# Attention's product with the values over four query blocks at once, with less descriptor scratch and another staging of branch A

## The chip, the cores and the metric

The kernel runs on one core of a Trainium2 chip. The metric is the device time of one execution in microseconds (us), given as the median of several runs. The kernel's engines are named as the profile names them: PE is TensorE's matmul row, PEld its weight loads, DVE is VectorE, ACT is ScalarE, POOL is GpSimd, and SP is the engine whose queue issues most of the DMAs.

## The reference

One layer of a hybrid encoder, on one sequence of 1024 tokens with 1024 channels, all in float32:

```python
h = rmsnorm(x, ln1_g) * (1 + sc1) + sh1
q, k, v, cb, cc, cx, ga, gb = split(h @ w_in)          # 16 heads of 64 channels for q, k, v
z = (rmsnorm(q) . rmsnorm(k)) / sqrt(64)               # strictly causal, 128-query blocks
A[t,s] = sigmoid(z_ts) * prod_{s<j<t} (1 - sigmoid(z_tj)),  s < t
y_a = A @ v                                            # per head
y_b = cb * causal_dwconv3(cc * cx)
merged = sigmoid(ga) * (y_a @ w_branch_a) + sigmoid(gb) * (y_b @ w_branch_b)
x = x + g1 * (merged @ w_out)
h = rmsnorm(x, ln2_g) * (1 + sc2) + sh2
x = x + g2 * ((silu(h @ w_gate) * (h @ w_up)) @ w_down)
```

sh1, sc1, g1, sh2, sc2 and g2 come from a product of silu(c) with a weight matrix.

## The kernel before

Every float32 product is made from a high and a low part of each operand, so a product of two split operands takes three matmuls (high by high, high by low, low by high). The stages follow each other: the input projections, attention together with branch B, branch A, the output projection, and the channel sub-layer with its two products. A matmul's moving operand is 512 columns wide nearly everywhere.

The change lies in the stage of attention. The generator `attention()` walks over 16 heads by 8 blocks of 128 queries; one pair of a head h and a block i is a step, s = 8h + i. In step s it issues

- the scores of its own block (`att_scores`, lines 921 and 922: `z` in two banks of PSUM, then ACT's sigmoid into a row tile `pt`, then a mask by POOL),
- the transposes of the block two steps earlier (`att_trans`, line 950: chunks of up to four 128x128 blocks into the PSUM tile `tr`; ACT copies the high part to `ath`, line 953, and DVE writes the low part to `atl`, line 954),
- the scan of its own block (`att_scan`, line 936 on DVE, and a product on POOL that finishes `pt`),
- in every second step the product with the values (`att_av`, lines 965 and 966), three steps behind (DAV = 3).

In `att_av` the stationary operand is `vt`, the 128 keys by 64 differences of neighbouring values, as 64 high and 64 low columns. The moving operand is a block of `ath` or `atl`: 128 keys by the queries of two blocks, 256 columns, and 128 columns for the last key block, which only the second of the two query blocks sees. The sums lie in the PSUM tile `o`. Two ACT instructions add the last value to the upper half (`otmp`, line 970), a DVE instruction adds the lower half (`oy`, line 972), and a DMA on SP's queue stores 64 channels by 256 queries in `d_ya` (line 974).

Each step's yields carry costs. The main loop adds them up and, in proportion, issues pieces of `fillers()` on PE: first conv B (the projection for cb, whose result is split into `ybh` and `ybl` and stored), then branch B's projection (lines 1026 to 1028, `pj`). A yield of 0 buys no piece before the last block; after it (`flush`), every yield buys 1.3 units, two pieces of three 512-column matmuls. PE's instructions, and those of DVE and POOL that belong to attention, are then chained in the order written (`in_order`); ACT, SP and the other DVE instructions are placed by the scheduler.

After attention, branch A's operand is read back: 16 loads `yr<-d_ya` on SP's queue (line 1173), each split by ACT (line 1176) and DVE into a tile `ya` that takes the place of an attention tile no longer used (`slots`). Pair (n, k) is half n of the queries and channel group k, that is heads 2k and 2k + 1; (1, 7) needs the last head's last product. Branch A multiplies these (`mm_ch`): its first two groups sum in the banks of `z`.

The pool `bp` holds the tiles of attention, `fp` those of fillers and staging, `fq` the tiles `ybh` and `ybl`. Meanwhile `mods_last` fetches 16 tiles `ad` of modulation weights by DMAs from POOL's queue, three buffers deep, and `preload_wo` splits the first weights of the output projection (line 1162) once those tiles are free.

Of the kernel before, what the change touches and what calls it, by code (L numbers as in the profile page):

```python
# [9 lines left out]
F32 = mybir.dt.float32  # L10
F32R = mybir.dt.float32r
AF = mybir.ActivationFunctionType
ALU = mybir.AluOpType
# [4 lines left out]
P = 128  # L18
# [4 lines left out]
DH = 64  # L23
# [7 lines left out]
def block_kernel(tc, x, x_t, cols, ada_1, ada_2, ada_row, w_q, w_kv, w_cg, w_a, w_b, w_o, w_g, w_u, w_d, out):  # L31
    nc = tc.nc
# [7 lines left out]
    def nm(s):  # L40
        uid[0] += 1
        return f"{s}_{uid[0]}"
# [29 lines left out]
    d_ya = [drp.tile([P, KT, 512], F32, name=f"d_ya{n}") for n in range(2)]  # L72
# [64 lines left out]
    pps = psA.enter_context(tc.tile_pool(name="psA", bufs=1, space=PSUM, reuse_waits="tile"))  # L137
# [759 lines left out]
    first_at = (at_tile("ath"), at_tile("atl"))  # L897
# [42 lines left out]
    def att_trans(h, i):  # L940
        pt, off = ptof.pop((h, i)), D - (i + 1) * P
        for b0 in range(0, i + 1, 4):
            nb = min(4, i + 1 - b0)
            key = (h, i // 2, b0 // 4)
            if key not in ats:
                ats[key] = (at_tile("ath"), at_tile("atl")) if ats else first_at
            th, tl = ats[key]
            tr = pps.tile([P, 512], F32, tag="tr", bufs=NTR, name=nm("tr"))
            for j in range(nb):
                nc.tensor.transpose(tr[:, j * P:(j + 1) * P], pt[:, off + (b0 + j) * P:off + (b0 + j + 1) * P], ident)  # L950
            c0 = (i % 2) * P
            src = tr[:, :nb * P].rearrange("p (j t) -> p j t", t=P)
            nc.scalar.activation(th[:, :nb, c0:c0 + P], src, AF.Copy)  # L953
            nc.vector.tensor_tensor(out=tl[:, :nb, c0:c0 + P], in0=src, in1=th[:, :nb, c0:c0 + P].bitcast(F32),  # L954
                                    op=ALU.subtract)
            yield F_T * nb

    def att_av(h, g):
        pr, e0 = h // 2, (h % 2) * DH
        vt = vts[h]  # L960
        o = pps.tile([P, 256], F32, tag="o", bufs=1, name=nm("o"))
        for j in range(2 * g + 2):
            c0 = P if j == 2 * g + 1 else 0
            th, tl = ats[h, g, j // 4]
            nc.tensor.matmul(o[:, c0:], vt[:, j, :], th[:, j % 4, c0:], start=(j == 0), stop=False)
            lastav[0] = nc.tensor.matmul(o[:, c0:], vt[:, j, :], tl[:, j % 4, c0:], start=False, stop=(j == 2 * g + 1))  # L966
        tmp = bp.tile([DH, 256], F32, tag="otmp", bufs=1, name=nm("otmp"))
        yv = bp.tile([DH, 256], F32, tag="oy", bufs=3, name=nm("oy"))
        for e in range(2):
            nc.scalar.activation(tmp[:, e * P:(e + 1) * P], o[:DH, e * P:(e + 1) * P], AF.Identity,  # L970
                                 bias=vlast[:, h, 2 * g + e:2 * g + e + 1])
        nc.vector.tensor_tensor(out=yv, in0=o[DH:], in1=tmp, op=ALU.add)
# [8 lines left out]
    def attention():  # L981

        steps = [(h, i) for h in range(H) for i in (LAST if h == H - 1 else ORDER)]
        for s in range(len(steps) + DAV):
# [27 lines left out]
            yield from av_  # L1012
# [118 lines left out]
    fqpool.close()  # L1131


    sml = ExitStack()
    mlp = sml.enter_context(tc.tile_pool(name="mlp", bufs=1, side="right", reuse_waits="tile"))
# [16 lines left out]
    def preload_wo():  # L1152

        wx = swx.enter_context(tc.tile_pool(name="wpx", bufs=1, side="right", reuse_waits="tile"))
        for j in range(3):
# [3 lines left out]
            for k in range(nk):  # L1159
# [7 lines left out]
    slots = [("va", 1), ("vb", 1), ("skl", 2), ("sq", 2), ("skh", 2), ("vt", 2), ("skl", 2), ("sq", 2), ("skh", 2),  # L1167
             ("ath", 3), ("atl", 3), ("ath", 3), ("atl", 3), ("ath", 3), ("atl", 3), ("vt", 2)]
    yah, yal = ([[None] * KT for n in range(2)] for e in range(2))
    with tc.high_priority():  # L1170
        for (tag, bufs), (n, k) in zip(slots, [(0, k) for k in range(7)] + [(1, 0), (1, 1), (1, 2), (0, 7)] + [(1, k) for k in range(3, 8)]):
            yr = fp.tile([P, 512], F32, tag="yr", bufs=3, name=nm("yr"))
            nc.sync.dma_start(yr, d_ya[n][:, k, :])
            ya2 = bp.tile([P, 2, 512], F32R, tag=tag, bufs=bufs, name=nm("ya"))
            h_, l_ = ya2[:, 0], ya2[:, 1]
            nc.scalar.activation(h_, yr, AF.Copy)
            tt(nc.vector, l_, yr, h_.bitcast(F32), ALU.subtract)
            yah[n][k], yal[n][k] = h_, l_
    mh, mlo = [None] * 2, [None] * 2
# [611 lines left out]
```

## Time and profile before

| what | value |
|---|---|
| median of 3 runs | 1793.41 us (1792.94 to 1793.71) |
| the profiled execution | 1792.41 us |
| its span, first to last instruction | 1790.4 us |
| granted TensorE clock | 1.000 |
| PE busy | 1782.5 us |
| PEld busy | 1485.4 us |
| DVE busy | 1273.5 us |
| ACT busy | 830.9 us |
| POOL busy | 345.0 us |

The median stands 1.0 us above the profiled execution, and that one 2.0 us above its span. Matmuls overlap in the pipeline: the profile gives each a start and a modelled end, so the mean duration of a 512-column matmul (389 ns) is longer than the distance from its start to the next start. What a matmul costs PE is that distance. Attention runs from 596 to 978 us of the span.

### The profile page before, as it was taken

The numbers are of one execution on the slowest core, as the hardware profiler recorded it, in microseconds if no ns is written. First come the engines' busy times: TensorE is split into PE (matmuls) and PEld (weight loads), VectorE is DVE, ScalarE is ACT, GpSimd is POOL, SyncE is SP. The second block draws the span as 40 slices with busy tenths as digits, with TensorE's granted clock in tenths as the row PEclk, the third lists the DMA queues.
The fourth block names the chain that finished last, engine by engine and source line by source line (L and its number), as shares of the span: only waits on it lengthen the run. The fifth ranks groups of instructions, "written<-read, shape, count | busy, mean of one in ns | idle before, by whom it ended". The sixth has DMA issues, their size and how long they took to land.

```text
span 1790.4 us, 24937 instructions
## 1 busy us (share of the span) xinstructions
PE 1782.5 (100%) x8611; PEld 1485.4 (83%) x8611; DVE 1273.5 (71%) x2030; ACT 830.9 (46%) x1555; POOL 345.0 (19%) x437
## 2 busy tenths in 40 slices
PE   9999999999999999999999999999999999999999
PEld 7888877888888888888888888888888888888887
DVE  6876586777874678777786864698867777644876
ACT  5534364333433567776675221764544444422321
POOL 0024334734231334333332100100000000000000
PEclk9999999999999999999999999999999999999999
DMA  9479654222634977796655856424534344389876
GB/s 383 162 248 381 240 185 165 77 94 100 225 130 147 298 197 191 218 324 172 166 136 176 308 194 212 129 95 169 208 130 148 147 183 157 137 316 345 276 236 220
DMA packets 165010, 359.09 MB, mean 201 GB/s; under 512 B 15538, under 2 KB 60938, under 8 KB 163732
## 3 DMA queue, kind: packets, MB, share of 16 engines
q1 hardware_dynamic: 128300, 289.65, 49.1%
q10 hardware_dynamic: 33096, 55.25, 8.7%
q0 software_dynamic: 3488, 12.59, 2.0%
q8 instruction: 69, 1.13, 0.3%
q14 instruction: 57, 0.47, 0.1%
HBM read 247.84 MB, written 109.62 MB: 200 GB/s over the span
## 4 chain that ended last, share of the span: by engine, by line
PE 96%; DMA 1%; DVE 1%; issue 0%; ACT 0%; POOL 0%; SPq 0%; POOLq 0%; DVEq 0%; ACTq 0%
PE e L129 8%; PE e L128 8%; PE e L127 8%; PE pj L127 7%; PE pj L128 7%; PE pj L129 7%; PE pj L294 7%; PE pj L1026 5%; PE pj L1028 5%; PE pj L1027 5%; PE e L1618 4%; PE e L1619 4%; PE e L1620 4%; PE tr L950 3%; PE o L966 2%; PE z L921 2%
## 5 line engine op out<-in xcount | busy, mean ns | idle before, releaser
L1234 ACT ACTIVATE whi<-raw 128x512 fp32r<-128x512 f32 x137 | 84.9, 628 | 160.6 <-PE e L128 99.8
L1235 DVE TENSOR_TENSOR wlo<-raw,whi 128x512 fp32r<-128x512 f32 x137 | 93.1, 687 | 70.6 <-ACT whi L1234 53.1
L133 POOL TENSOR_TENSOR pt<-pt 128x63 f32<-128x63 f32 (+7 forms) x128 | 101.6, 794 | 212.1 <-DVE pt L936 195.7
L128 PE MATMUL e<-big,whi 128*128 128x512 f32 x352 | 136.9, 389 | 0.0
L127 PE MATMUL e<-big,whi 128*128 128x512 f32 x352 | 136.5, 390 | 0.0
L129 PE MATMUL e<-big,wlo 128*128 128x512 f32 x352 | 136.1, 389 | 0.0
L294 PE MATMUL pj<-whi,big 128*128 128x512 f32 x448 | 132.6, 393 | 0.6 <-ACT big L263 0.4
L133 DVE TENSOR_TENSOR c<-pj,c 128x512 f32<-128x512 f32 x140 | 93.7, 684 | 53.9 <-PE pj L129 53.3
L954 DVE TENSOR_TENSOR atl<-tr,ath 128x512 fp32r<-128x512 f32 (+1 forms) x192 | 104.1, 553 | 35.6 <-ACT ath L953 34.2
L127 PE MATMUL pj<-big,whi 128*128 128x512 f32 x320 | 124.9, 390 | 0.0
L129 PE MATMUL pj<-big,wlo 128*128 128x512 f32 x320 | 124.7, 390 | 0.0
L128 PE MATMUL pj<-big,whi 128*128 128x512 f32 x320 | 124.6, 389 | 0.0
L1619 PE MATMUL e<-wlo,f 128*128 128x512 f32 (+1 forms) x319 | 121.9, 382 | 0.0
L1618 PE MATMUL e<-whi,f 128*128 128x512 f32 (+1 forms) x319 | 121.7, 382 | 0.0
L1620 PE MATMUL e<-whi,f 128*128 128x512 f32 (+1 forms) x319 | 121.6, 382 | 0.0
L923 ACT ACTIVATE pt<-z,rq 128x128 f32<-128x128 f32 (+1 forms) x192 | 107.2, 578 | 26.3 <-PE z L922 23.8
L524 ACT ACTIVATE whi<-raw 128x512 fp32r<-128x512 f32 x108 | 67.5, 629 | 109.0 <-PE pj L128 54.3
L133 DVE TENSOR_TENSOR wlo<-raw,whi 128x512 fp32r<-128x512 f32 x108 | 89.4, 831 | 36.2 <-ACT whi L524 36.1
L1026 PE MATMUL pj<-big,whi 128*128 128x512 f32 x256 | 113.3, 442 | 0.0
L953 ACT ACTIVATE ath<-tr 128x512 fp32r<-128x512 f32 (+1 forms) x192 | 93.2, 488 | 31.8 <-PE tr L950 30.8
L127 PE MATMUL e<-rh,whi 128*128 128x512 f32 x264 | 102.7, 389 | 0.0
L128 PE MATMUL e<-rl,whi 128*128 128x512 f32 x264 | 102.7, 389 | 0.0
(304 smaller groups left out, 4756.1 us busy)
## 6 DMA issues: line engine op xcount, KB each, us to landing
f<-d_f SPq DMA_DIRECT2D x77, 512.0 KB, 4.2
d_f<-fs SPq DMA_DIRECT2D x70, 512.0 KB, 2.6
raw<-w_cg SPq DMA_DIRECT2D x40, 512.0 KB, 4.1
raw<-w_u SPq DMA_DIRECT2D x26, 512.0 KB, 4.5
raw<-w_g SPq DMA_DIRECT2D x25, 512.0 KB, 3.4
raw<-w_kv SPq DMA_DIRECT2D x20, 512.0 KB, 5.2
ld<-ada SPq DMA_DIRECT2D x16, 512.0 KB, 8.7
d_t<-ts SPq DMA_DIRECT2D x16, 512.0 KB, 6.7
```

The lines of the kernel that those rows point to most:

```text
L127: nc.tensor.matmul(ps, wh[:, k, :], fh[:, k, :], start=(k == 0 and not onto), stop=False, skip_group_check=onto)
L128: nc.tensor.matmul(ps, wh[:, k, :], fl[:, k, :], start=False, stop=False, skip_group_check=onto)
L129: last = nc.tensor.matmul(ps, wl[:, k, :], fh[:, k, :], start=False, stop=(k == 3), skip_group_check=onto)
L133: eng.tensor_tensor(out=out, in0=a, in1=b, op=op)
L294: nc.tensor.matmul(ps, a, b, start=(k == 0 and q == 0), stop=(k == KT - 1 and q == 2))
L923: nc.scalar.activation(pt[:, off + s0:off + s0 + m], z[:, :m], AF.Sigmoid, scale=rq[:, 1, i, h:h + 1])
L953: nc.scalar.activation(th[:, :nb, c0:c0 + P], src, AF.Copy)
L954: nc.vector.tensor_tensor(out=tl[:, :nb, c0:c0 + P], in0=src, in1=th[:, :nb, c0:c0 + P].bitcast(F32), op=ALU.subtract)
L1026: nc.tensor.matmul(ps, wh, rh_, start=(k == 0), stop=False)
L1618: nc.tensor.matmul(o, sh, w[0][:, c], start=(j == 0), stop=False)
L1619: nc.tensor.matmul(o, sh, w[1][:, c], start=False, stop=False)
L1620: nc.tensor.matmul(o, sl, w[0][:, c], start=False, stop=(j == NJ - 1))
```

## The change

`att_av` now takes four query blocks at once. It is called for i = 3 and i = 7 of a head in place of i = 1, 3, 5 and 7. For key blocks that all four query blocks see, the moving operand has 512 columns; for the four diagonal key blocks it has 512, 384, 256 and 128. It is issued in pieces of two key blocks, with yields of 0 between. In the steps with s % 8 = 6 the first piece stands behind the first chunk of transposes, the rest at the end of the step. For the second half of a head the first two pieces stand at the end of the step with s % 8 = 2, the third piece behind the first chunk of transposes of the next step, and the last piece at that step's end. After the last block everything stands in one step.

The transposed blocks lie in new tiles: `afh` and `afl` for the keys all four blocks see (16 x 128 columns, one buffer each), `ath` and `atl` for the diagonal part (13 x 128 columns, packed, two buffers each). Four ACT instructions write the result's tile `oy` itself, a DVE instruction of 512 columns adds the lower half in place, and one DMA stores 64 channels by 512 queries.

The staging tile `yr` leaves `fp` (three buffers) and uses the buffers of `ybh` and `ybl` in turn (four); the slots for `ya` are cut from the new tiles. The pool of `ybh` and `ybl` is closed behind the staging. The kernel asks for a scratch of 2048 bytes for dynamic DMA descriptors in place of the default.

```diff
-    def at_tile(tag):
-        return bp.tile([P, 4, 256], F32R, tag=tag, bufs=3, name=nm(tag))
+    def at_tile(full):
+        return tuple(bp.tile([P, (16 if full else 13) * P], F32R, tag=t_, bufs=1 if full else 2, name=nm(t_))
+                     for t_ in (("afh", "afl") if full else ("ath", "atl")))
...
     def att_trans(h, i):
         pt, off = ptof.pop((h, i)), D - (i + 1) * P
+        c = i % 4
         for b0 in range(0, i + 1, 4):
             nb = min(4, i + 1 - b0)
-            key = (h, i // 2, b0 // 4)
+            full = i // 4 > b0 // 4
+            key = (h, i // 4, full)
...
-            c0 = (i % 2) * P
+            u, f = (4, 0) if full else (3, c // 3)
+            th, tl = (t_[:, f * P:(4 * u + f) * P].rearrange("p (j t) -> p j t", t=u * P)[:, :nb, (c - f) * P:(c - f + 1) * P]
+                      for t_ in ats[key])
             src = tr[:, :nb * P].rearrange("p (j t) -> p j t", t=P)
-            nc.scalar.activation(th[:, :nb, c0:c0 + P], src, AF.Copy)
-            nc.vector.tensor_tensor(out=tl[:, :nb, c0:c0 + P], in0=src, in1=th[:, :nb, c0:c0 + P].bitcast(F32),
-                                    op=ALU.subtract)
+            nc.scalar.activation(th, src, AF.Copy)
+            nc.vector.tensor_tensor(out=tl, in0=src, in1=th.bitcast(F32), op=ALU.subtract)
             yield F_T * nb
 
     def att_av(h, g):
         pr, e0 = h // 2, (h % 2) * DH
         vt = vts[h]
-        o = pps.tile([P, 256], F32, tag="o", bufs=1, name=nm("o"))
-        for j in range(2 * g + 2):
-            c0 = P if j == 2 * g + 1 else 0
-            th, tl = ats[h, g, j // 4]
-            nc.tensor.matmul(o[:, c0:], vt[:, j, :], th[:, j % 4, c0:], start=(j == 0), stop=False)
-            lastav[0] = nc.tensor.matmul(o[:, c0:], vt[:, j, :], tl[:, j % 4, c0:], start=False, stop=(j == 2 * g + 1))
-        tmp = bp.tile([DH, 256], F32, tag="otmp", bufs=1, name=nm("otmp"))
-        yv = bp.tile([DH, 256], F32, tag="oy", bufs=3, name=nm("oy"))
-        for e in range(2):
-            nc.scalar.activation(tmp[:, e * P:(e + 1) * P], o[:DH, e * P:(e + 1) * P], AF.Identity,
-                                 bias=vlast[:, h, 2 * g + e:2 * g + e + 1])
-        nc.vector.tensor_tensor(out=yv, in0=o[DH:], in1=tmp, op=ALU.add)
-        hf, c0 = g // 2, (g % 2) * 256
-        nc.sync.dma_start(d_ya[hf][e0:e0 + DH, pr, c0:c0 + 256], yv)
+        o = pps.tile([P, 512], F32, tag="o", bufs=1, name=nm("o"))
+        for j in range(4 * g + 4):
+            full, d = j < 4 * g, j % 4
+            c0 = 0 if full else d * P
+            for e, t in enumerate(ats[h, g, full]):
+                lastav[0] = nc.tensor.matmul(o[:, c0:], vt[:, j, :], t[:, 4 * d * P:4 * d * P + 512 - c0],
+                                             start=(j + e == 0), stop=(j == 4 * g + 3 and e == 1))
+            if j % 2 and j < 4 * g + 3:
+                yield 0
+        yv = bp.tile([DH, 512], F32, tag="oy", bufs=2, name=nm("oy"))
+        for e in range(4):
+            nc.scalar.activation(yv[:, e * P:(e + 1) * P], o[:DH, e * P:(e + 1) * P], AF.Identity,
+                                 bias=vlast[:, h, 4 * g + e:4 * g + e + 1])
+        nc.vector.tensor_tensor(out=yv, in0=o[DH:], in1=yv, op=ALU.add)
+        nc.sync.dma_start(d_ya[g][e0:e0 + DH, pr, :], yv)
         yield 0
...
     def attention():
...
-            av_ = att_av(steps[s - DAV][0], steps[s - DAV][1] // 2) if s >= DAV and s % 2 != DAV % 2 else iter(())
+            if s >= DAV and steps[s - DAV][1] % 4 == 3:
+                av.append(att_av(steps[s - DAV][0], steps[s - DAV][1] // 4))
+            mid = s % 8 not in (2,)
             yield from itertools.islice(tr_, 1)
-            if s >= DAV and steps[s - DAV][1] == 5:
-                yield from av_
+            if av and mid:
+                yield from itertools.islice(av[0], 1)
             yield from tr_
             if s < len(steps):
                 att_scan(*steps[s])
-            yield from av_
+            for a_ in av:
+                yield from (a_ if s % 8 not in (2,) or s >= len(steps) else itertools.islice(a_, 2))
+            if s % 8 not in (2,):
+                av.clear()
...
-    slots = [("va", 1), ("vb", 1), ("skl", 2), ("sq", 2), ("skh", 2), ("vt", 2), ("skl", 2), ("sq", 2), ("skh", 2),
-             ("ath", 3), ("atl", 3), ("ath", 3), ("atl", 3), ("ath", 3), ("atl", 3), ("vt", 2)]
+    def ya_slots():
...
+        for t_ in at_tile(False):
+            yield t_[:, :1024].rearrange("p (e t) -> p e t", t=512)
+        for t_ in at_tile(True):
+            t_ = t_.rearrange("p (e t) -> p e t", t=512)
+            yield t_[:, :2]
+            yield t_[:, 2:]
+        yield bp.tile([P, 2, 512], F32R, tag="vt", bufs=2, name=nm("ya"))
...
-            yr = fp.tile([P, 512], F32, tag="yr", bufs=3, name=nm("yr"))
+            yr = fq.tile([P, 512], F32, tag=("ybh", "ybl")[j % 2], bufs=2, name=nm("yr"))
...
-    nc = bacc.Bacc("TRN2", target_bir_lowering=False, num_devices=1)
+    nc = bacc.Bacc("TRN2", target_bir_lowering=False, num_devices=1, dynamic_dma_scratch_size=2048)
```

More of the change, by code (lines that the diff above doesn't have):

```diff
@@ L896, in block_kernel @@
     first_vl = bp.tile([9, 512], F32, tag="vl", bufs=1, name=nm("vl"))
-    first_at = (at_tile("ath"), at_tile("atl"))
+    first_at = {True: at_tile(True), False: at_tile(False)}
     first_va = v_tile(1)
@@ L941, in att_trans @@
         pt, off = ptof.pop((h, i)), D - (i + 1) * P
+        c = i % 4
         for b0 in range(0, i + 1, 4):
             nb = min(4, i + 1 - b0)
-            key = (h, i // 2, b0 // 4)
+            full = i // 4 > b0 // 4
+            key = (h, i // 4, full)
             if key not in ats:
-                ats[key] = (at_tile("ath"), at_tile("atl")) if ats else first_at
-            th, tl = ats[key]
+                ats[key] = first_at.pop(full) if full in first_at else at_tile(full)
             tr = pps.tile([P, 512], F32, tag="tr", bufs=NTR, name=nm("tr"))
@@ L981, in attention @@
     def attention():
+        av = []
         steps = [(h, i) for h in range(H) for i in (LAST if h == H - 1 else ORDER)]
@@ L1164, in preload_wo @@
                 w_pre.append((hi, lo))
-    slots = [("va", 1), ("vb", 1), ("skl", 2), ("sq", 2), ("skh", 2), ("vt", 2), ("skl", 2), ("sq", 2), ("skh", 2),
-             ("ath", 3), ("atl", 3), ("ath", 3), ("atl", 3), ("ath", 3), ("atl", 3), ("vt", 2)]
+    def ya_slots():
+        for tag, bufs in (("va", 1), ("vb", 1), ("skl", 2), ("sq", 2), ("skh", 2), ("vt", 2), ("skl", 2), ("sq", 2), ("skh", 2)):
+            yield bp.tile([P, 2, 512], F32R, tag=tag, bufs=bufs, name=nm("ya"))
+        for t_ in at_tile(False):
[5 more added lines that the diff above has]
+        yield bp.tile([P, 2, 512], F32R, tag="vt", bufs=2, name=nm("ya"))
     yah, yal = ([[None] * KT for n in range(2)] for e in range(2))
     with tc.high_priority():
-        for (tag, bufs), (n, k) in zip(slots, [(0, k) for k in range(7)] + [(1, 0), (1, 1), (1, 2), (0, 7)] + [(1, k) for k in range(3, 8)]):
-            yr = fp.tile([P, 512], F32, tag="yr", bufs=3, name=nm("yr"))
+        for j, (ya2, (n, k)) in enumerate(zip(ya_slots(), [(0, k) for k in range(7)] + [(1, 0), (1, 1), (1, 2), (0, 7)] + [(1, k) for k in range(3, 8)])):
+            yr = fq.tile([P, 512], F32, tag=("ybh", "ybl")[j % 2], bufs=2, name=nm("yr"))
             nc.sync.dma_start(yr, d_ya[n][:, k, :])
-            ya2 = bp.tile([P, 2, 512], F32R, tag=tag, bufs=bufs, name=nm("ya"))
             h_, l_ = ya2[:, 0], ya2[:, 1]
@@ L1178, in block_kernel @@
             yah[n][k], yal[n][k] = h_, l_
+    fqpool.close()
+    sml = ExitStack()
+    mlp = sml.enter_context(tc.tile_pool(name="mlp", bufs=1, side="right", reuse_waits="tile"))
     mh, mlo = [None] * 2, [None] * 2
```

3 lines of the change are left out of this document (removed).

## The prediction

> **What bounds the kernel now.** I read the page's busy times first, then the stages, then single matmuls in order of time.
>
> ```profile
> span 1790.4 us, 24937 instructions
> PE 1782.5 (100%) x8611; PEld 1485.4 (83%) x8611; DVE 1273.5 (71%) x2030; ACT 830.9 (46%) x1555; POOL 345.0 (19%) x437
> ```
>
> PE is busy in all but 7.9 us of the span. The windows, whose columns are the busy time of PE, PEld, DVE, ACT and POOL with counts, the clock, the DMA share and GB/s, say the same of attention and of its end:
>
> ```profile
> 760.00:800.00 40.00, 39.89 (x249) 34.81 (x248) 32.18 (x55) 28.27 (x64) 15.87 (x28) 1.00 0.98 342
> 960.00:1000.00 40.00, 40.00 (x196) 33.51 (x196) 26.46 (x45) 15.41 (x27) 4.92 (x8) 1.00 0.73 243
> ```
>
> The clock is full, DVE (32.2 of 40) is next. Since nothing but PE's queue sets the end, a us less of PE's work anywhere is a us less of time, provided that no new wait appears. But busy here hides how dense the stream is, because modelled ends overlap the next start. So I read the distance between starts. Attention, PE's instructions in order of time, first column the start:
>
> ```profile
> 776.12 0.28 PE L965 MATMUL o<-ath,vt 128*128 128x256 f32 x1
> ...
> 777.29 0.22 PE L965 MATMUL o<-ath,vt 128*128 128x128 f32 x1
> ...
> 781.04 0.40 PE L1026 MATMUL pj<-big,whi 128*128 128x512 f32 x1
> ...
> 781.73 0.34 PE L921 MATMUL z<-skh,sqt 128*128 128x384 f32 x1
> 781.91 0.34 PE L922 MATMUL z<-skl,sqt 128*128 128x384 f32 x1
> 782.09 0.27 PE L950 MATMUL tr<-dm,pt 128*128 128x128 f32 x1
> ...
> 782.31 0.28 PE L966 MATMUL o<-atl,vt 128*128 128x256 f32 x1
> ...
> 783.87 0.22 PE L965 MATMUL o<-ath,vt 128*128 128x128 f32 x1
> 783.93 0.28 PE L966 MATMUL o<-atl,vt 128*128 128x128 f32 x1
> 784.04 0.45 PE L921 MATMUL z<-skh,sqt 128*128 128x512 f32 x1
> 784.33 0.40 PE L922 MATMUL z<-skl,sqt 128*128 128x512 f32 x1
> 784.56 0.38 PE L950 MATMUL tr<-dm,pt 128*128 128x128 f32 x2
> ```
>
> - 256 columns: ten between 776.12 and 777.29, thirteen between 782.31 and 783.87: 23 in 2.73 us, 0.1187 us each (0.117 and 0.120).
> - 512 columns: three between 781.04 and 781.73, 0.230 each. That is less than two of 256 (0.237).
> - 384 columns: 0.180.
> - The pair of 128 columns that ends each product: from its start to the transposes after the two scores are 0.69 us; less two at 0.230, the pair costs 0.230, as much as a whole matmul of 512 columns. Part of it shows up only in the score behind it (784.04 to 784.33 is 0.29), so reading the pair's own rows alone (0.17) would miss that.
>
> **The change, part by part.** *The product.* Per head, before: calls g = 0 to 3 with 2(2g + 1) matmuls of 256 columns, 32 in all, and four pairs of 128. After: 12 of 512 (two on the diagonals of each half, eight before the second), four of 384, four of 256, two pairs. The columns are the same, 9216 per head; 640 matmuls become 384, 64 pairs become 32. Two groups confirm the old number:
>
> ```profile
> L965 PE MATMUL o<-ath,vt 128*128 128x256 f32 x256 | 67.0, 293 | 0.0
> L966 PE MATMUL o<-atl,vt 128*128 128x256 f32 x256 | 64.3, 283 | 0.3 <-DVE atl L954 0.3
> ```
>
> Before: 32 x 0.1187 + 4 x 0.230 = 4.72 us per head. After: 12 x 0.230 + 4 x 0.180 + 4 x 0.1187 + 2 x 0.230 = 4.42. The difference of 0.30 times 16 heads is **4.8 us**. Bounds: outside attention, 512 columns go faster,
>
> ```profile
> 981.58 0.39 PE L1026 MATMUL pj<-ya,whi 128*128 128x512 f32 x1
> ...
> 983.62 0.39 PE L1026 MATMUL pj<-ya,whi 128*128 128x512 f32 x1
> ```
>
> nine in 2.04 us, 0.227; with that (the pair then is 0.236) the gain is 5.7. With all 256s at the faster 0.117 it is 4.1. I take 4.8, from rows of attention itself.
>
> The Trainium skill, "TensorE: Matmul & The Clock Gate", section "Back-to-back issue gap", has the warm distance as columns/2.4 plus 2.5 ns; an estimate by it is 55.9 + 7.1 us before (512 x 0.1092, 128 x 0.0558) and 62.4 after, a gain of only 0.6 us. The trace disagrees: 0.1187 for 256 columns where that has 0.109, and 0.230 for a pair where it has 0.112.
>
> *Waits of the product.* One wait of o for atl (0.3 us, in the row above) should go: the first piece now stands more than a chunk of transposes and its fillers behind the split that it needs, the second half's pieces a whole step. I leave it out of the sum, against small new ones.
>
> *Getting it out of PSUM.* ACT keeps 128 instructions, four in a row instead of two; DVE has 32 of 512 columns in place of 64 of 256.
>
> ```profile
> 765.30 0.60 ACT L970 ACTIVATE otmp<-o,vlast 64x128 f32<-64x128 f32 x2
> L972 DVE TENSOR_TENSOR oy<-o,otmp 64x256 f32<-64x256 f32 x64 | 27.3, 426 | 20.6 <-ACT otmp L970 14.8 <-DMA sqt<-d_q 2.8 <-PE tr L950 1.3
> L954 DVE TENSOR_TENSOR atl<-tr,ath 128x512 fp32r<-128x512 f32 x96 | 65.6, 686 | 20.5 <-ACT ath L953 19.8
> ```
>
> At 0.69 us (the nearest row of 512 columns) DVE needs 22 us; now it is 27. Both lie beside PE and count nothing, unless DVE's later work is held up: DVE keeps its order, and behind the add stand the next splits and the scan, which POOL finishes and the transposes wait for. Each add moves by 0.6 us (two more ACT instructions) and lasts 0.26 longer. That is the main risk, below. The bank o is asked for again only four steps later.
>
> *Transposes* keep their counts; only addresses change. *Stores* on SP: 32 in place of 64, nothing waits for them but the staging. *Staging:* the same 16 loads over four buffers in place of three; those are free once conv B, the fillers' first part, is over. First use, and the end of the stage:
>
> ```profile
> L1176 ACT ACTIVATE ya<-yr x16: 614/624/635, 923.7 to 987.7; 128x512 fp32r<-128x512 f32 x16
> L1028 PE MATMUL z<-ya,wlo x16: 389/389/400, 962.0 to 989.5; 128*128 128x512 f32 x16
> 977.53 0.27 PE L966 MATMUL o<-atl,vt 128*128 128x128 f32 x1
> ```
>
> From the last o (977.5) to the last split (started 987.7) PE does left-over fillers and branch A's first groups. After the change the last product is twice as long with two pieces of fillers behind each part, and its exit 0.9 us longer (0.6 + 0.26); so (1, 7) comes some 3.4 us later against the same cover: half the fillers of the flush between the four parts (2 to 3 us) and 0.9. The two z groups (48 matmuls, 11 us) can stretch over that, so I count nothing; if they don't, up to 3.4 us.
>
> *Places in memory.* Attention's tiles grow, so the first loads land elsewhere, on other tiles of the stage before.
>
> ```profile
> 587.70 0.57 SPq L843 DMA_DIRECT2D skl<-d_k  x1
> skl<-d_k SPq DMA_DIRECT2D x32, 256.0 KB, 6.5
> 596.06 0.22 PE L921 MATMUL z<-skh,sqt 128*128 128x128 f32 x1
> ```
>
> The last load, issued at 587.7, has landed by about 594.2; the first score starts at 596.06. 1.9 us of slack cover a later issue. Taken at 0; beyond the slack it costs one for one, and no gain is in it, since PE is dense there.
>
> *Descriptor scratch.* It concerns DMAs from POOL's queue: the 16 loads `ad`, a broadcast and 8 stores. With three buffers at most three loads are under way; if fewer fit, loads come one by one.
>
> ```profile
> L644 POOL DMA_DIRECT2D ad<-ada x16: 527/527/538, 967.3 to 1032.9; - x16
> ad<-ada POOLq DMA_DIRECT2D x16, 512.0 KB, 5.7
> L1162 ACT ACTIVATE whi<-raw x5: 612/616/632, 1049.6 to 1056.1; 128x512 fp32r<-128x512 f32 x5
> L1028 PE MATMUL pj<-ya,wlo x112: 389/389/395, 982.0 to 1063.1; 128*128 128x512 f32 x112
> ```
>
> I take 0: loads are spread over 66 us. The upper bound is a rival. The Trainium skill, "DMA: Bandwidth & Descriptors", section "The descriptor swizzle", has 9 read and 9 write descriptors per engine for a transfer over 128 partitions; its table of terms has 16 bytes for each, and an estimate from both is some 14 such loads in 2048 bytes. No run here shows the ring's filling.
>
> **Sum:** -4.8 us. Against its own execution (1792.4 us, span 1790.4) that is 1787.6; the median stands 1.0 above that execution, so 1793.4 - 4.8 = **1788.6 us**.
>
> **The rivals.** *No change beyond 0.2% (3.6 us), which is about what a measurement here can tell from none.* The mechanism is the end of the stage: 3.4 us uncovered leave a gain of 1.4, 1792.0 us. For it: the chain after the last o is longer. Against: PE has no gap there today and the z groups are left. Small stalls elsewhere lead to the same place. A variant is that matmuls cost their columns alone: then nothing is gained, 1793.4; the distances above speak against it, and it gets 0.03. The Trainium skill's section on the issue gap, named above, would make that 1792.8.
>
> *Slower: DVE's order.* One place in time order, with the rows of ACT, DVE, POOL and PE:
>
> ```profile
> 771.02 0.67 ACT L970 ACTIVATE otmp<-o,vlast 64x128 f32<-64x128 f32 x2 [0.61 <-PE o L966]
> 773.81 0.43 DVE L972 TENSOR_TENSOR oy<-o,otmp 64x256 f32<-64x256 f32 x1
> 775.91 1.21 DVE L936 TENSOR_TENSOR_SCAN pt<-pt 128x512 f32<-128x512 f32 x1
> 777.27 1.04 POOL L133 TENSOR_TENSOR pt<-pt 128x511 f32<-128x511 f32 x1 [2.16 <-DVE pt L936]
> 778.77 0.60 PE L950 MATMUL tr<-dm,pt 128*128 128x128 f32 x4
> ```
>
> POOL is done at 778.31, the transposes start at 778.77: 0.46 us of slack. If both delays (0.86) reached the scan at all 32 adds, 0.40 x 32 = 12.8 us come back: 1793.4 - 4.8 + 12.8 = 1801.4. It decides from 0.26 us of stall at each add (8.4 us in all). Against: here DVE came to the add 2.1 us after ACT had finished (771.69), so ACT's two more instructions hide and only 0.26 reaches the scan, under the slack; and half the adds disappear. For: today's stall is small but there,
>
> ```profile
> PE tr L950 <- POOL pt L133: 0.9, 2, 0.5
> ```
>
> *Slower: the ring.* Loads one by one take 16 x (5.7 + 0.53) = 100 us from 967.3, to 1067 in place of 1038.6 (1032.9 + 5.7). The weights now split at 1049.6 to 1056.1 would be 28 us late, of which some 6 are slack, as branch A's last matmul starts at 1063.1 and both halves of the last split take 1.3: 1793.4 - 4.8 + 22 = 1810.6.
>
> **How the numbers follow.** Forecast, gain of 3.6 or more: 0.57. Within 0.2%: end of stage and small stalls 0.28, columns alone 0.03. DVE's order: 0.09; ring: 0.03. So faster 0.57, same 0.31, slower 0.12. The range goes from 1786.0 (5.7 by the bound, the waits of 0.3 and 0.9 gone, 0.5 for the spread of the runs) up to 1794.5, through the end-of-stage case; some 2 in 10 lie outside, mostly above. The likeliest case alone spans 1786.5 to 1789.8.
>
> **What would show it.** Groups o with 192 matmuls of 512 columns, 0.230 apart, and 32 pairs; attention about 4.8 us shorter from the first score to the last transposes; PE at 40.0 of 40 in its windows and through the end; no more waits of tr for POOL; `ad` issues still spread to about 1030. Wrong, if 512-column products stand 0.237 apart or more, if PE waits grow at the transposes behind an add, or if a gap opens behind the last o.

## The result, and the profile after

The changed kernel takes 1802.92 us (median of 4 runs, 1802.14 to 1803.18), the kernel before 1793.56 (4 runs, 1792.94 to 1793.94). The ratio is 1.0052, with a 95% interval of 1.0034 to 1.0069: 9.4 us slower, where 4.8 us less had been forecast. The profiled execution takes 1802.75 us, its span is 1800.7, 10.3 longer than before. The page of the changed kernel begins:

```profile
span 1800.7 us, 24252 instructions
PE 1781.3 (99%) x8355; PEld 1471.2 (82%) x8355; DVE 1267.0 (70%) x1998; ACT 827.7 (46%) x1555; POOL 342.0 (19%) x437
```

PE has 256 matmuls fewer, as planned, and stands idle for 19.4 us in place of 7.9. In the kernel before, PE was busy for 39.6 to 40.0 of 40 us in the windows of attention. One of them (the same columns as in the prediction):

```profile
640.00:680.00 40.00, 40.00 (x247) 34.87 (x247) 31.74 (x55) 29.66 (x68) 16.14 (x30) 1.00 0.68 189
```

After:

```profile
640.00:680.00 40.00, 37.06 (x201) 30.31 (x200) 27.36 (x47) 24.97 (x58) 14.00 (x27) 1.00 0.68 187
...
920.00:960.00 40.00, 38.48 (x215) 32.17 (x214) 31.00 (x52) 27.31 (x64) 14.03 (x28) 1.00 0.55 152
960.00:1000.00 40.00, 40.00 (x195) 33.08 (x195) 23.65 (x36) 19.28 (x39) 7.03 (x11) 1.00 0.64 210
```

The clock is full, and no other engine has become the bound: in the first two of these windows DVE and ACT do less than before (before, DVE had 31.7 and 32.2 us there, ACT 29.7 and 29.9). The holes lie inside attention. Its first and last starts, from the instructions of the tile `tr`, before and then after:

```profile
L950 PE MATMUL tr<-dm,pt x576: 270/272/332, 598.8 to 971.8; 128*128 128x128 f32 x192
```

```profile
L952 PE MATMUL tr<-dm,pt x576: 270/272/331, 598.8 to 980.8; 128*128 128x128 f32 x192
```

From the first to the last transposes it is 373.0 us before and 382.0 after: 9.0 of the 10.3 us. Another 1.4 stand between the last transposes and the output projection. All that comes before attention, and all from the output projection on, agrees within 0.1 us.

The waits of PE in the changed kernel say for what:

```profile
PE tr L952 <- POOL pt L133: 9.5, 12, 1.4
...
PE z L922 <- ACT pt L924: 1.6, 3, 1.0
```

The first row had stood at 0.9 us in two waits. Nine of the twelve, 7.9 of the 9.5 us, are the first transposes of block 7, the longest block of a head: they wait in 9 of 16 heads. (Two, 0.7 us together, stand at block 4, and one of 0.9 us at block 1 of the first head; the two of before stood at blocks 1 and 2 of the first head, none at block 7.) One of the nine, in the sixth head, in order of time (a bracket is idle time and what ended it):

```profile
729.17 0.39 PE L969 MATMUL o<-ath,vt 128*128 128x512 f32 x1
729.40 0.40 PE L969 MATMUL o<-atl,vt 128*128 128x512 f32 x1
729.63 0.34 PE L969 MATMUL o<-ath,vt 128*128 128x384 f32 x1
729.81 0.34 PE L969 MATMUL o<-atl,vt 128*128 128x384 f32 x1
...
730.51 0.45 PE L922 MATMUL z<-skh,sqt 128*128 128x512 f32 x1
...
730.71 1.13 ACT L975 ACTIVATE oy<-o,vlast 64x128 f32<-64x128 f32 x4
...
731.73 1.25 ACT L924 ACTIVATE pt<-z,rq 128x512 f32<-128x512 f32 x2
...
732.01 0.69 DVE L977 TENSOR_TENSOR oy<-o,oy 64x512 f32<-64x512 f32 x1
...
733.52 0.69 DVE L1054 TENSOR_TENSOR cy<-pj,cy 128x512 f32<-128x512 f32 x1 [0.81 <-PE pj L1038]
...
735.66 1.22 DVE L937 TENSOR_TENSOR_SCAN pt<-pt 128x512 f32<-128x512 f32 x1
...
736.79 0.67 DVE L1058 TENSOR_TENSOR ybl<-cy,ybh 128x512 fp32r<-128x512 f32 x1
...
737.02 1.33 POOL L133 TENSOR_TENSOR pt<-pt 128x511 f32<-128x511 f32 x1 [3.71 <-DVE pt L937]
...
738.41 0.66 PE L952 MATMUL tr<-dm,pt 128*128 128x128 f32 x4 [1.42 <-POOL pt L133]
```

Read it from block 7's scores at 730.51. The chain runs over ACT's sigmoid, DVE's scan and POOL's product, which ends at 738.35, 7.84 us later. PE ran out of work 1.42 us ahead of 738.41, at 736.99: it had 6.48 us of work for a chain of 7.84. The same head in the kernel before:

```profile
724.41 0.45 PE L921 MATMUL z<-skh,sqt 128*128 128x512 f32 x1
...
729.47 0.28 PE L965 MATMUL o<-ath,vt 128*128 128x256 f32 x1
729.56 1.22 DVE L936 TENSOR_TENSOR_SCAN pt<-pt 128x512 f32<-128x512 f32 x1
...
730.83 0.52 PE L950 MATMUL tr<-dm,pt 128*128 128x128 f32 x3
730.92 1.33 POOL L133 TENSOR_TENSOR pt<-pt 128x511 f32<-128x511 f32 x1 [3.39 <-DVE pt L936]
...
732.31 0.66 PE L950 MATMUL tr<-dm,pt 128*128 128x128 f32 x4
```

The chain is just as long: POOL is done 7.84 us after the scores. But PE had 7.90 us of work beside it, and 1.36 us of that, from 729.47 to 730.83, is block 5's product with the values, issued in the step after block 7's scores. (At the place that the prediction showed, the same product took 1.35 us, from 776.12 to 777.47.) In the changed kernel block 5's columns belong to the product of the second half, three steps after block 7.

### The profile page after: what moved, and what is told of

Same layout as the page of the kernel before. It is cut to its first block, busy times and chain, and to the rows that moved or that the text cites. A ratio compares the mean times of both kernels' runs of the same rounds, so it can differ in the third digit from the quotient of the medians.

```text
span 1800.7 us, 24252 instructions
## 1 busy us (share of the span) xinstructions
PE 1781.3 (99%) x8355; PEld 1471.2 (82%) x8355; DVE 1267.0 (70%) x1998; ACT 827.7 (46%) x1555; POOL 342.0 (19%) x437
## 4 chain that ended last, share of the span: by engine, by line
PE 91%; DVE 3%; DMA 2%; ACT 2%; issue 1%; POOL 1%; SPq 0%; POOLq 0%; ACTq 0%; DVEq 0%
PE e L129 8%; PE e L127 8%; PE e L128 8%; PE pj L127 7%; PE pj L129 7%; PE pj L128 7%; PE pj L294 7%; PE pj L1036 4%; PE e L1635 4%; PE e L1634 4%; PE e L1636 4%; PE pj L1038 4%; PE pj L1037 4%; PE o L969 4%; PE tr L952 3%; PE e L1371 2%
## 5 line engine op out<-in xcount | busy, mean ns | idle before, releaser
L133 POOL TENSOR_TENSOR pt<-pt 128x63 f32<-128x63 f32 (+7 forms) x128 | 96.4, 753 | 215.6 <-DVE pt L937 193.3
L952 PE MATMUL tr<-dm,pt 128*128 128x128 f32 x576 | 95.3, 274 | 9.6 <-POOL pt L133 9.5
L129 PE MATMUL e<-rh,wlo 128*128 128x512 f32 x264 | 102.0, 389 | 0.0
```

Of the source, the lines that this page charges most:

```text
L129: last = nc.tensor.matmul(ps, wl[:, k, :], fh[:, k, :], start=False, stop=(k == 3), skip_group_check=onto)
L133: eng.tensor_tensor(out=out, in0=a, in1=b, op=op)
```

## The experiments

The theory: block 7's chain from scores to transposes has lost its cover, since the product of block 5 left the step between (*lost cover*). The rivals: the exit of a product, four ACT instructions and a longer add, delays block 7's scan (*exit*); the descriptor scratch; the end of the stage.

**The scratch alone.**

```diff
-    nc = bacc.Bacc("TRN2", target_bir_lowering=False, num_devices=1)
+    nc = bacc.Bacc("TRN2", target_bir_lowering=False, num_devices=1, dynamic_dma_scratch_size=2048)
```

> The kernel before with nothing changed but the descriptor scratch of 2048 bytes. Theory 1 (cover: the product of block 5 no longer stands between the scores of block 7 and its transposes, so PE reaches those transposes before POOL has finished the row): the scratch has no part in it, 1793.5 us within 1.5. Theory 2 (the block of four ACT instructions and the longer add hold up DVE's scan): the same, 1793.5. Rival 3 (scratch or the places of tiles in memory): some or all of the 9.4 us, 1796 to 1803.

1793.37 us, ratio 0.9997 (0.9987 to 1.0006). The scratch has no part in it. The loads `ad` on POOL's queue keep their pace:

```profile
L644 POOL DMA_DIRECT2D ad<-ada x16: 527/527/539, 967.6 to 1033.2; - x16
```

**The kernel before, with one product moved.** Products of 256 columns stay; block 5's goes from step 8h + 8 to the end of the step after it. This needs a fourth buffer of `ath` and `atl`, and the small scratch.

```diff
-                yield from av_
+                held, av_ = av_, iter(())
...
+            if s % 8 == 1:
+                yield from held
```

> The kernel before, products of 256 columns and their exits as they were; only block 5's product moves from the step with s % 8 = 0 behind the transposes of the step with s % 8 = 1 (one more buffer for the transposed blocks, room for it from the scratch of 2048 bytes). Theory 1: 1.4 us of PE's work leaves the stretch before the first transposes of block 7, which had 1.17 us of slack at the median, so those transposes wait 0.3 to 0.7 us in most heads: 1797 to 1804. Theory 2: the exits are as before, no more waits, 1793.5.

1812.88 us, ratio 1.0104 (1.0089 to 1.0119). The waits of PE:

```profile
PE tr L950 <- POOL pt L133: 8.8, 10, 1.4
PE o L965 <- DVE oy L972: 6.7, 10, 0.7
```

The first row is much like the changed kernel's (9.5, 12, 1.4), with none of its wide products and none of its exits; eight of these ten waits, 7.6 us, stand at block 7. The second row is made by the experiment: the one bank `o` is asked for again a step later, while the held product's sums are still in it. So moving that product is enough for the wait at block 7. The time is above the expected one (1797 to 1804); of the 19.7 us over the kernel before, the second row is 6.7, and 4 to 5 stand in neither row.

**POOL's product of block 7 left out** in the changed kernel (every second element of that block's rows stays unfinished), so that the transposes need the scan alone.

```diff
-        tt(nc.gpsimd, mid, mid, pt[:, slice(off + 2, D - 1, 2)], ALU.mult)
+        if i != 7:
+            tt(nc.gpsimd, mid, mid, pt[:, slice(off + 2, D - 1, 2)], ALU.mult)
```

> The changed kernel with POOL's product left out for block 7 alone (its odd positions are not finished), so that its transposes wait for DVE's scan and no longer for POOL. Theory 1: the chain from block 7's scores to its transposes is 1.3 us shorter, so the 9.7 us of wait fall to 0 to 2 us: 1792 to 1796. If the wait were of another origin (a bank, a buffer): 1803.

1792.91 us, ratio 0.9995 (0.9985 to 1.0004): 10 us below the changed kernel, from sixteen instructions of 1.04 to 1.33 us on the least busy of these engines. The waits for POOL that are left stand at blocks 1, 2 and 4, none at block 7:

```profile
PE tr L953 <- POOL pt L133: 1.5, 4, 0.4
```

**Work put in the gap, or the exit cut.** The first kernel buys about 1.4 us of fillers in each step 8h, out of those bought elsewhere. The second replaces the exit by one ACT instruction of 0.68 us and no addition on DVE; it leaves out the lower half of the sums and three of each four last values.

```diff
+            if s % 8 == 0 and 0 < s < len(steps):
+                yield F_W
```

> The changed kernel with its products where they are, but the steps with s % 8 = 0 buy about two more pieces of fillers (1.4 us) behind their first transposes, where block 5's product stood before; all other steps get fewer. Theory 1 (cover): any work of PE will do, the wait of block 7's transposes (9.7 us) falls below 3 us: 1794 to 1798, the rest being waits that thinner fillers open elsewhere. If the width of the product or the memory were the cause: 1803.

```diff
-        for e in range(4):
-            nc.scalar.activation(yv[:, e * P:(e + 1) * P], o[:DH, e * P:(e + 1) * P], AF.Identity,
-                                 bias=vlast[:, h, 4 * g + e:4 * g + e + 1])
-        nc.vector.tensor_tensor(out=yv, in0=o[DH:], in1=yv, op=ALU.add)
+        nc.scalar.activation(yv, o[:DH], AF.Identity, bias=vlast[:, h, 4 * g:4 * g + 1])
```

> The changed kernel, but the product leaves PSUM by one ACT instruction of 512 columns with one block's bias, and DVE's add of the lower half is left out. Order and place of the matmuls are as in the changed kernel. Theory 1: the stretch of PE's work is as short as it was; the sigmoid comes at most 0.4 us earlier per head, so most of the wait at block 7's transposes stays: 1797 to 1803. Theory 2: nothing of the exit stands before the scan any more, the wait goes, 1789 to 1794.

Fillers: 1796.84 us, ratio 1.0017 (1.0008 to 1.0026). Short exit: 1796.36, ratio 1.0016 (1.0007 to 1.0025). The waits, first with fillers, then with the short exit:

```profile
PE tr L952 <- POOL pt L133: 2.8, 5, 1.3
PE z L922 <- ACT pt L924: 2.2, 6, 0.6
```

```profile
PE tr L952 <- POOL pt L133: 7.5, 10, 1.4
```

Fillers in the gap, too, take most of block 7's wait away, as lost cover has it: 1.7 us in two heads are left of 7.9 in nine. With the short exit 6.3 us in eight heads are left, so *exit* is the lesser part of its cause. Yet the kernel with the short exit is 6.6 us faster than the changed one: the exit has a price of its own, most of it in other places (below).

**The first half's product given back to the gap.** The changed kernel issues it in step 6 of its head. First held to step 7, then held whole to the next head's step 0, then piece by piece, each right behind a step's first transposes (steps 7 and 0; 2 to 5 for the other half). The edits:

```diff
-            mid = s % 8 not in (2,)
+            n_end = {2: 2, 6: 0}.get(s % 8) if s < len(steps) else None
+            mid = s % 8 not in (2, 6,)
...
+                yield from (a_ if n_end is None else itertools.islice(a_, n_end))
...
```

```diff
+            n_end = {2: 2, 6: 0, 7: 0}.get(s % 8) if s < len(steps) else None
+            mid = s % 8 not in (2, 6, 7)
...
+                yield from (av[0] if s % 8 == 0 else itertools.islice(av[0], 1))
...
```

```diff
+            if av and s % 8 != 6:
+                yield from (av[0] if s % 8 == 2 and s >= len(steps) else itertools.islice(av[0], 1))
+                if s % 8 in (0, 5):
+                    av.clear()
...
```

> The changed kernel with the first half's product held back by one step: it stands in the step with s % 8 = 7, between the scores of block 7 and its transposes. Theory 1: the wait of block 7's transposes (9.7 us over the heads) goes, the product stays 4 to 6 us cheaper than before: 1788 to 1791; waits of block 5's transposes may appear, since their stretch loses 1.3 us and had 1.8 of slack. Theory 2: the add moves behind block 7's scan, so the wait goes as well, 1788 to 1792: the two are not told apart here. Rival 3: no change, 1803.

> The changed kernel with the first half's product (1.3 us) held back to the step with s % 8 = 0, behind the first transposes, as block 5's stood before. Theory 1: block 7's transposes no longer wait (below 1 us in all); but no product stands any more between the scores of block 6 and its transposes, which had 1.0 us of slack with 0.94 us of product there: those wait up to 0.3 us a head, 1 to 5 us in all. Time 1790 to 1797.

> The changed kernel with the products spread out, one piece of two key blocks a step, always behind the first transposes: the first half's two pieces in the steps with s % 8 = 7 and 0, the second half's four in those with 2, 3, 4 and 5. Theory 1: each stretch of two steps holds 0.5 to 1.9 us of product, as it did before, so the waits fall back to about 3 us and the cheaper product (4 to 6 us) shows in the time: 1787 to 1791. If the change costs something besides the order of PE's work, it stays above 1793.

Step 7: 1795.97 us, ratio 1.0014 (1.0004 to 1.0024). Step 0: 1799.31, 1.0029 (1.0018 to 1.0040). Piece by piece: 1799.06, 1.0030 (1.0018 to 1.0041). All three are above what theory 1 gave; the third came out as its alternative had it, that the change costs something besides the order of PE's work. The waits, in this order:

```profile
PE tr L952 <- POOL pt L133: 2.8, 7, 0.5
...
PE o L969 <- ACT afh L957: 1.6, 1, 1.6
```

```profile
PE tr L952 <- POOL pt L133: 5.1, 11, 1.0
```

```profile
PE tr L952 <- POOL pt L133: 6.3, 18, 0.9
```

In step 7 the product covers block 7 in all but three heads (1.4 us of waits for POOL). In step 0 it covers block 7 fully, but block 6, before it, then waits in 7 heads (3.7 of the 5.1 us). Piece by piece, block 5 waits in 14 of 16 heads (3.9 of the 6.3 us): there the exit's add is issued ahead of its scan. In these runs each block needs the product beside its own chain.

The wait of `o` in the first fence is a single one, in the tail: the last head's first half was held back too, its store came later, and ACT stood behind a copy of staging that waited for its load:

```profile
972.60 0.63 ACT L1190 ACTIVATE atl<-yr 128x512 fp32r<-128x512 f32 x1 [9.77 <-DMA yr<-d_ya]
973.14 0.58 ACT L957 ACTIVATE afh<-tr 128x512 fp32r<-128x512 f32 x1
```

**Three more placements**, with the second half's product at the end of step 2 (the first half's in steps 7 and 0), split over steps 2 to 4, or at the end of step 2 with the first half's in step 7:

```diff
+            mid, end = ({0: 1, 7: 1}, {2: 9}) if s < len(steps) else ({0: 1}, {2: 9})
...
```

```diff
+            mid, end = ({0: 1, 3: 1, 7: 1}, {2: 2, 4: 1}) if s < len(steps) else ({0: 1}, {2: 9})
...
```

```diff
+            mid, end = ({7: 1}, {2: 9, 7: 1}) if s < len(steps) else ({0: 1}, {2: 9})
...
```

> The changed kernel with the first half's two pieces behind the first transposes of the steps with s % 8 = 7 and 0, and the whole second half at the end of the step with s % 8 = 2, as the last product stood before. Theory 1 (cover) with what the spread run showed (an add ahead of a scan costs too): no product is ahead of a scan but in step 0; block 7 waits 1 to 2 us in all, block 4, whose stretch is empty (0.47 us before), about 1, scores that wait for ACT about 1: 1790 to 1795.

> As the run beside it, but the second half in parts: two pieces at the end of the step with s % 8 = 2, one behind the first transposes of step 3, the last with the exit at the end of step 4, where a product's exit stood before. Theory 1: every stretch holds at least as much product as before or nearly so, block 4 has its 0.47 us again and no add stands ahead of a scan but in step 0: waits 3 to 5 us in all, 1788 to 1791.

> The changed kernel with the first half whole in the step with s % 8 = 7 and the second half whole at the end of the step with s % 8 = 2. Theory 1: as the first run with step 7 (1796.0, block 7 waiting 3.1 us in all), but the exit of the second half is one step earlier, so the waits of scores for ACT and of block 4 (2.4 us there) go: 1792 to 1795.

1798.23 us (ratio 1.0025, 1.0015 to 1.0035), 1797.95 (1.0024, 1.0015 to 1.0033) and 1798.16 (1.0033, 1.0022 to 1.0044). None helps: all are slower than expected and than step 7 alone. With the second half at the end of step 2, the exit stands on ACT ahead of a sigmoid, and block 4's scores wait for ACT in 14 heads (the row is alike in the first and the third):

```profile
PE z L922 <- ACT pt L924: 2.5, 14, 0.2
```

**What is left of the loss.** The versions that cover block 7 by the first half's product had all held back the last head's first half as well. Four kernels on top of step 7's placement: the last head as in the changed kernel; besides this the exit cut as above (it leaves out the same parts); block 7's scan ahead of its step's second chunk of transposes in place of the cut; and 0.7 us of fillers in step 8h with that scan.

```diff
+            hold = {2: 2, 6: 0} if s < len(steps) - 8 else {2: 2}
+            n_end = hold.get(s % 8) if s < len(steps) else None
+            mid = s % 8 not in hold
...
```

> The changed kernel with the first half's product held to step 7 of its head, except in the last head, where it stands in step 6 as in the changed kernel. Theory 1 (the tail's 1.75 us of waits, behind ACT's copy that waited for a load, came from holding back the last head's first half): that wait is gone, the stretch from the last transposes to the output projection falls from 96.0 to 92 to 93 us, block 7 still waits some 2.5 to 3 us in all, and the time is 1791.5 to 1794. Rival (the tail is longer for another reason): the stretch stays at 95 to 96 us and the time at 1795 to 1797.

```diff
+        nc.scalar.activation(yv, o[:DH], AF.Identity, bias=vlast[:, h, 4 * g:4 * g + 1])
```

> As e12, but with one ACT instruction of 512 columns in place of four and no addition by DVE. It leaves out the lower half of the sums and three of each four last values. Theory 1 (beside block 7's lost cover, the exit's own work delays scores and transposes): the remaining waits of PE inside attention fall by 3 us or more, and the time is 3 to 6 us below e12. Rival (the exit's work is beside PE, as the prediction had it): within 1.5 us of e12.

```diff
+            if s % 8 == 7 and s < len(steps):
+                att_scan(*steps[s])
...
+            if s < len(steps) and s % 8 != 7:
...
```

> As e12, but block 7's scan is issued ahead of the second chunk of transposes of its step, so on DVE it stands ahead of that chunk's subtraction. Theory 1 (what is left of block 7's wait is DVE's queue ahead of the scan): block 7's waits fall from some 3 us to below 1 us, and the time is 1 to 3 us below e12. Rival (the scan waits for ACT's sigmoid, not for DVE): block 7's waits stay as they are, and the subtraction behind the scan delays block 6's low parts: no change or up to 2 us slower than e12.

```diff
+    F_Z, F_T, F_S, F_W = 0.2, 0.3, 0.05, 1.2
...
+            if s % 8 == 0 and 0 < s < len(steps):
+                yield F_W
```

> As e14, with about 0.7 us of fillers bought between block 7's scores and its transposes in each head, taken from the other places in proportion. If lost cover is all that is left in attention, block 7's waits are nil and the time is 0 to 2 us below e14; if the cover that the fillers leave elsewhere was needed there, waits of the scores for ACT grow by as much and the time is that of e14 or above.

Against 1794.11 us for the kernel before: 1794.20 (ratio 1.0002, 0.9993 to 1.0011), 1790.22 (0.9978, 0.9969 to 0.9987), 1793.60 (0.9997, 0.9988 to 1.0006) and 1793.34 (0.9997, 0.9988 to 1.0006). Their waits, in this order:

```profile
PE tr L952 <- POOL pt L133: 3.1, 6, 1.0
...
PE z L922 <- ACT pt L924: 0.7, 2, 0.3
```

```profile
PE tr L952 <- POOL pt L133: 2.4, 5, 0.8
```

```profile
PE tr L952 <- POOL pt L133: 2.1, 5, 0.6
```

```profile
PE z L922 <- ACT pt L924: 1.3, 4, 0.3
PE tr L952 <- POOL pt L133: 1.1, 3, 0.4
```

The single wait of `o` is gone with the last head's first half back in its place. Placement alone brings the changed kernel back to the time of before, 8.7 us of the 9.4. With the exit cut, it is 4.0 us below the kernel with the same placement: so the exit, which the prediction had beside PE, is not all beside it. (That kernel also drops work that the kernel before has; its 1790.22 is a measure of the exit, and no version to be had.) The earlier scan takes block 7's waits for POOL from 1.4 us in three heads to 0.5 in one, and with the fillers they are gone, while the scores wait for ACT for 1.3 us in place of 0.7. The exit cut came out as expected; the first kernel is 0.2 us above its range, the third 0.6 us below the first in place of 1 to 3, and the fourth can't be told from the third. Neither of the last two can be told from the kernel before, so no version that does all the work is faster than it.

## Why the prediction was wrong

**The product's own saving was about right.** Its distances in the rows above are 0.23 for 512 columns (729.17, 729.40, 729.63) and 0.18 for 384. Every distance between two starts, from the first score to the last product, charged to the matmul that begins it, with what is over the usual distance left out as a stall, gives 72.9 us for the products before (61.7 for 512 matmuls of 256 columns, 11.15 for 128 of 128) and 68.6 after (192 of 512 columns 44.3, 64 each of 384, 256 and 128 columns 11.3, 7.5 and 5.5). That is 4.3 us less against a term of 4.8 with bounds of 4.1 to 5.7. (With every distance counted whole the sums are 75.9 and 71.7, and the gain is 4.1.) The part of a pair that shows up in the score behind it isn't in these sums. The Trainium skill, "TensorE: Matmul & The Clock Gate", section "Back-to-back issue gap", gives its warm distance, columns/2.4 plus 2.5 ns, for a matmul by itself; by that estimate the gain was 0.6 us, and here, too, the trace disagrees.

**The step that failed** is the sentence that a us less of PE's work anywhere is a us less of time, and with it the product's term, which counted a total per head and gave no price to where the work stands. The condition "provided that no new wait appears" was looked for, inside attention, at the exit alone. The products were two things: work, and the cover of the chain beside which they stood. Moving block 5's product out of step 8h took 1.35 us of cover from a chain whose slack the prediction had measured at one place, 0.46 us, and quoted the rows to see it: the product from 776.12 to 777.47 stands between block 7's scores and its transposes at 778.77. Less 0.46, that would be 0.9 us of wait per head, 14 in 16 heads. But the slack, from the end of POOL's product to the transposes, differs from head to head: in the kernel before it goes from 0.06 to 1.99 us in the first fifteen heads and is 5.57 in the last. What 1.35 us exceeds it by, summed over the heads, is 7.7 us, all but 0.1 of it in nine heads. Those are the nine that wait in the changed kernel, for 7.9 us.

**The rival "DVE's order"** named the right place and nearly the right time (1801.4), but mostly for the wrong reason; that the time fits is luck. By it the exit's two more ACT instructions and longer add push the scan back. But in the rows above the scan starts 5.15 us after block 7's scores in both kernels (735.66 less 730.51, 729.56 less 724.41 in the same head), and with the exit cut 6.3 of block 7's 7.9 us of waiting stay. In the first, the third and the last head the scan does come later than before, by 1.25, 0.97 and 1.44 us; the last has slack enough and doesn't wait. Where the add does stand ahead of a scan, as piece by piece, the rival's mechanism shows: in the fourth head of that run the add lasts from 677.72 to 678.41, block 5's scan starts at 678.33 behind it, and the transposes wait 0.48 us.

**Getting it out of PSUM** was counted nothing; that was the second miss. The changed kernel's instructions, whole run:

```profile
L975 ACT ACTIVATE oy<-o,vlast 64x128 f32<-64x128 f32 x128 | 36.6, 355 | 10.3 <-PE o L969 9.3
L977 DVE TENSOR_TENSOR oy<-o,oy 64x512 f32<-64x512 f32 x32 | 22.2, 693 | 15.6 <-ACT oy L975 15.0
```

The busy sums were right (22 us on DVE, 128 instructions on ACT). What they miss is that four ACT instructions in a row hold ACT's queue for 1.13 us (730.71) while block 7's sigmoid stands behind them, at 731.73. Shortening the exit was worth 4.0 us with the product in step 7 and 6.6 in the changed kernel. In the former, 2.9 us of it are stalls: distances between PE's starts that exceed the usual one for their shapes by over 40 ns add up to 8.9 us with the exit and 6.0 without it. (By the same count it is 2.9 before and 15.4 in the changed kernel.) What is usual is a choice: the median over the same three shapes in a row gives 9.4 and 6.1, 3.3 before and 16.7 in the changed kernel. By the latter count the short exit saves 5.6 us of stalls in the changed kernel: 3.0 at the scores of blocks 0 and 5, which wait for ACT, 1.5 at block 7's transposes and 0.9 at block 4's. Both edits shorten ACT's part and drop DVE's add together, so which of the two costs more is not shown.

**The balance of the changed kernel** in attention and up to the output projection: +12.5 us of stalls, -4.3 of products, and +2.2 that I didn't assign, in a stretch that is 10.4 us longer (by the other count of stalls +13.4). With the product in step 7 of all heads but the last the stalls exceed those of before by 6.0 us, most of it at block 7 and at block 5's scores, which wait for ACT; they eat the 4.3 us. So the saving is there, and stalls beside the chains take it back.

**The small terms.** Scratch at 0: right, by the run of the scratch alone. The estimate from the Trainium skill, "DMA: Bandwidth & Descriptors", section "The descriptor swizzle", of some 14 loads in 2048 bytes is not contradicted by that run: the loads kept their pace. The section counts the descriptors of a transfer of 1 MiB, and these loads are 512 KB; how full the ring was, no run showed. Places in memory at 0: right, the first score starts at 596.1 in both. The sign of a stall, two waits of `tr` for POOL, was read at block 7's place, but they stood at blocks 1 and 2 of the first head. The tail at 0 up to 3.4: it cost 1.4. The bounds of the range came from the terms of the sum and left this loss out, as no term had a price for cover.

## What to carry to other kernels

When PE runs without gaps beside a chain through other engines, a piece of PE's work has two values: its duration, and the wait that it covers where it stands. Before moving it, measure for each chain, and at each of its repeats, the time from its start to its end and PE's work in between; a move is free only where the slack is larger than the piece moved. Larger and fewer pieces cost less on PE but cover less evenly, and what they hand to ACT or DVE comes in one block, ahead of whatever stands behind it in the queue.

## What was not expected of the hardware

POOL's product of block 7 takes 1.04 us in 13 of 16 heads and 1.33 in three, before and after alike. In those three a DVE instruction that reads two operands from SBUF is under way when it starts (`ybl<-cy,ybh` above, 736.79 to 737.46); beside a DVE instruction with an operand in PSUM, such as a split of `tr`, it takes 1.04. The other way round, DVE is the one held up. The last head of the changed kernel, with the rows of DVE and POOL:

```profile
971.45 0.68 DVE L133 TENSOR_TENSOR wlo<-raw,whi 128x512 fp32r<-128x512 f32 x1
...
973.75 1.04 POOL L133 TENSOR_TENSOR pt<-pt 128x511 f32<-128x511 f32 x1 [6.11 <-DVE pt L937]
...
974.10 1.24 DVE L133 TENSOR_TENSOR wlo<-raw,whi 128x512 fp32r<-128x512 f32 x1
```

The same split, of two operands in SBUF, takes 1.24 us behind POOL's start in place of 0.68. The Trainium skill, "SBUF — State Buffer", section "Who interferes with whom", has it that a DVE instruction with two inputs in SBUF shares a read port with POOL and that whichever issues second waits for the first. The rows agree that the second one lasts longer, by 0.29 and 0.56 us; they don't show it as waiting. On a chain without slack, 0.29 us of this kind would reach PE; no run shows that by itself.
